# Sums of weight blocks by DMA: spread over the front in smaller pieces, products reordered, sums of F moved to VectorE

## The chip, the cores and the metric

The kernel runs on one core of a Trainium2 chip. The metric is the device time of one execution in microseconds; the time stated is the median of three runs. A separate profiled execution gives the traces.

## The reference

One layer of a hybrid trunk over 512 tokens and 16 learned ones (528 rows, width 1024): an input projection feeds an RWKV-7 recurrence (8 heads of 64), a forgetting attention (8 heads of 64) and gates; then comes an MLP.

```python
u = rmsnorm(h, norm_mix)
proj = u @ w_in
gates = sigmoid(proj[..., C_RW + C_FX:] + b_gate)
y_rw = rwkv7_branch(proj[..., :C_RW], ...)      # S = S*diag(w) + (S a) b^T + v k^T ; y = S r
y_fx = fox_branch(proj[..., C_RW:C_RW + C_FX], ...)  # causal softmax with a decay of F = cumsum(log_f)
merged = gates[..., :D] * (y_rw @ w_out_rw) + gates[..., D:] * (y_fx @ w_out_fx)
h = h + merged @ w_o
z = rmsnorm(h, norm_mlp)
h = h + square(relu(z @ w_up)) @ w_down         # 1024 -> 4096 -> 1024
```

## The kernel before

Every large product is made in three passes: each float32 operand is split into a high part (`whi`, `fhi`, a conversion on ScalarE) and the rest (`wlo`, `flo`, a subtraction on VectorE or GpSimd), and TensorE adds high x high, high x low and low x high.

**The front** (up to about 515 us of the span) does the projections, the recurrence and the attention. A planner (`Turns`, `Clock`) writes the order of TensorE's instructions: several streams (the recurrence's chain, rank 0; its preparation, rank 1; attention, 2; its features, 3; group norms, 4; projections and gates, 8; the sums of the weights, 9) are asked in turn, and the lowest rank whose inputs are due on the planner's clock goes next. TensorE keeps the order so written. The other engines' instructions are ordered by a scheduler, which may take an instruction early if nothing that it reads is missing. The recurrence handles two groups of two head pairs: for each pair keys, `rows`, `scores` (`psr`, L761) and turned keys (`pbt`), then for the group a triangular inverse (`Ain`, `AX`, `tmp`, L784 to L858) and a chain of nine chunks (`pch`, L887 to L919). The projections load a block of weights (`wraw`, two halves of 128x512 from `in_win`, L438), convert it (L447 on ScalarE, L448 on GpSimd) and multiply it (L476); there are four buffers each of `wraw`, `whi` and `wlo`, so two blocks.

**The MLP's second product** is made from 2x2 blocks by Winograd's form of Strassen's scheme: seven products in place of eight. F = square(relu(z w_up)) is cut in four blocks by rows (two of 256 tokens) and by inner index (the halves of a pair of 128 columns); `w_down` into B11, B12, B22, B21. The right factors need four sums of the weights, T1 to T4 (`tsum`), which do not depend on the data: `weight_sums` makes them in HBM by DMA during the front, a copy issued by ScalarE and an accumulating DMA issued by GpSimd for each, in pieces of 512 rows (1 MB): T1 = B11 + B12, T3 = B12 + B22, T2 = B22 + T1, T4 = B21 + T2, in the signs that the blocks hold. The left factors need S1 to S4, sums of blocks of F, made per pair in `left_factors` (L1146 to L1155) by GpSimd.

The inner dimension goes in three slices of 6, 6 and 4 pairs. In each slice the up products (`up_part`, L1138) write F's blocks (`R`, `up_evac`), `left_factors` converts seven left factors (`fhi`, `flo`), and then come seven products over the slice's pairs (L1204): A11 B11, S2 T2, S3 T3, S1 T1, A12 B21, S4 B22, A22 T4. Two of them (`x6`, `x7`) gather in PSUM over all slices (`pd`), two in `v1` and `v5`, and three are added to the result `hres`. In the last slice the gathered ones are combined, with GpSimd adding `v1` and `v5` to `hres` (L1230 to L1239), and the result is stored.

Of the kernel before, what the change touches and what calls it, by code (L numbers as in the profile page):

```python
# [9 lines left out]
F32 = mybir.dt.float32  # L10
# [18 lines left out]
SLICES = (6, 6, 4)  # L29
# [120 lines left out]
class Turns:  # L150
# [4 lines left out]
    ROOM = {0: 0.0, 1: 0.8, 2: 1.5, 3: 1.5, 4: 2.5, 8: 0.5, 9: 0.0}  # L155
# [32 lines left out]
def kernel(ctx, tc, ht, x, win, par, cst, gain, lora, wout, wo, wup, wdn, out, dbg=None):  # L188
# [78 lines left out]
    tsum = [dr.tile([2048, 512], F32, name=f"tsum{i}") for i in range(4)]  # L267

    with ExitStack() as st:
# [136 lines left out]
        opened = act(gf, gf, AF.Tanh, scale=0.5)  # L406
# [592 lines left out]
        def weight_sums():  # L999

            def part(t, c):
                return t[512 * c:512 * c + 512].rearrange("(a b) c -> a (b c)", b=4)

            t1, t2, t3, t4 = tsum
            b11, b12, b22, b21 = (wdn[i] for i in range(4))
            steps = []
            for c in range(4):
                for dst, src in ((t1, b11), (t3, b12), (t2, b22), (t4, b21)):
                    steps.append((dst, src, c, False))
                for dst, src in ((t1, b12), (t3, b22), (t2, t1), (t4, t2)):  # L1010
                    steps.append((dst, src, c, True))
            for n, (dst, src, c, adds) in enumerate(steps):
                yield lambda: 50.0 + 11.0 * n
                if adds:
                    nc.gpsimd.dma_start(part(dst, c), part(src, c), accum_op=ALU.add, max_dma_last_dim=8192)
# [115 lines left out]
    with ExitStack() as st:  # L1131
# [15 lines left out]
        def left_factors(fhi, flo, j, R):  # L1147

            a11, a12, a22, s1, s2, s3, s4, a21 = (R[:, i, :] for i in range(8))
# [4 lines left out]
            A.copy(fhi[:, j], R[:, :7])  # L1154
            V.tensor_tensor(flo[:, j], R[:, :7], fhi[:, j].bitcast(F32), ALU.subtract)  # L1155

        def right_factors(src):

            return [load_h(src[128 * b:128 * b + 128], V, "w", (4, 4, 4)) for b in range(2)]

        A11, A12, A22, S1, S2, S3, S4 = range(7)
        B11, B22, B21, T1, T2, T3, T4 = wdn[0], wdn[2], wdn[3], *tsum
# [4 lines left out]
        p0 = 0  # L1167
        for n_pairs in SLICES:
# [27 lines left out]
            def product(x, left, right, start, stop):  # L1196

                for j in range(0, n_pairs, 2):
                    r0 = 128 * (p0 + j)
                    w = right_factors(right[r0:r0 + 256])  # L1200
                    final = left in (A12, S4, A22) and last and j == n_pairs - 2
                    for i, b in [(i, b) for i in range(2) for b in range(2)] if final else [(i, b) for b in range(2) for i in range(2)]:
                        for n, (a, c) in enumerate(passes((fhi, flo), w[b])):
                            mm(x[i], a[:, j + b, left, 128 * i:128 * i + 128], c, start=start and j + b == 0 and n == 0,  # L1204
                               stop=stop and j + b == n_pairs - 1 and n == 2)

            def gathered(v, left, right):
                x = [ppo() for i in range(2)]
                product(x, left, right, True, True)
                for i in range(2):  # L1210
                    if first:
                        A.copy(v[:, i], x[i])
                    else:
                        V.tensor_tensor(v[:, i], v[:, i], x[i], ALU.add)

            def added(a, b, left, right, op):
                x = [ppo() for i in range(2)]
                product(x, left, right, True, True)
                for i in range(2):
                    h = hr[a][b][:, i]  # L1220
                    V.tensor_tensor(h, h, x[i], op)
                    if last:
                        r0 = 256 * a + 128 * i
                        nc.sync.dma_start(out[r0:r0 + 128, 512 * b:512 * b + 512], h)

            gathered(v1, A11, B11)
            product(x6, S2, T2, first, last)
            product(x7, S3, T3, first, last)
            if last:
                G.tensor_tensor(hr[0][0], hr[0][0], v1, ALU.add)  # L1230
                for i in range(2):
                    V.tensor_tensor(v1[:, i], x6[i], v1[:, i], ALU.subtract)
                G.tensor_tensor(hr[0][1], hr[0][1], v1, ALU.add)
                for i in range(2):
                    V.tensor_tensor(v1[:, i], v1[:, i], x7[i], ALU.subtract)
            gathered(v5, S1, T1)
            if last:
                G.tensor_tensor(hr[0][1], hr[0][1], v5, ALU.subtract)
                G.tensor_tensor(hr[1][0], hr[1][0], v1, ALU.subtract)  # L1239
                for i in range(2):  # L1240
                    h = hr[1][1][:, i]
                    V.tensor_tensor(h, h, v1[:, i], ALU.add)
                    V.tensor_tensor(h, h, v5[:, i], ALU.subtract)
                    r0 = 256 + 128 * i
                    nc.sync.dma_start(out[r0:r0 + 128, 512:], h)
            added(0, 0, A12, B21, ALU.add)
            added(0, 1, S4, B22, ALU.subtract)
            added(1, 0, A22, T4, ALU.add)
            p0 += n_pairs

# [76 lines left out]
```

## Time and profile before

| | us |
|---|---|
| median of three runs | 954.82 (953.65 to 956.38) |
| the profiled execution | 957.5 |
| its span | 955.6 |
| TensorE matmul busy | 866.4 (91%) |
| VectorE busy | 590.1 (62%) |
| ScalarE busy | 460.1 (48%) |
| GpSimd (POOL) busy | 238.3 (25%) |
| mean granted TensorE clock | 0.962 |

In the views PE is TensorE, PEld its weight loads, DVE VectorE, ACT ScalarE, POOL GpSimd, SP the engine that issues most DMAs. A row of the timeline or of the chain of waits has the start in us, the duration in us, and what ran, with "out<-in" by the program's names; in brackets stands the idle time before it and who ended it. A row of the waits has who waited for whom, us in total, times, and the longest. A row of the stages has the stretch and its length, then the busy time of each engine with its number of instructions, the granted TensorE clock, the mean busy share of the 16 DMA engines and GB/s. L12 is line 12 of the kernel.

### The profile page before, as it was taken

What the parts mean: (1) busy time and instruction counts of PE and PEld (TensorE: products, weight loads), DVE (VectorE), ACT (ScalarE), POOL (GpSimd) and SP (SyncE); (2) the same over time, 40 slices, a digit from 0 to 9 for tenths busy, and PEclk for the clock granted to TensorE, in tenths of its full rate; (3) what the DMA queues carried; (4) which work ended last, traced back from release to release, by engine and by line L of the source; (5) the groups of instructions that cost most, each with busy time, mean ns of one, the idle gap of its engine ahead of it and who ended that gap; (6) DMA issues with size and microseconds to landing.
All of it is one profiled execution on the core that took longest, in us unless ns stands there. A gap on an engine that the chain in (4) does not pass through costs nothing.

```text
span 955.6 us, 15670 instructions
## 1 busy us (share of the span) xinstructions
PE 866.4 (91%) x5868; PEld 700.5 (73%) x5868; DVE 590.1 (62%) x1102; ACT 460.1 (48%) x923; POOL 238.3 (25%) x229
## 2 busy tenths in 40 slices
PE   6668794689999989999998999999999999999987
PEld 4566783476788768767686887888788887888865
DVE  7857443745588779446447766446556466564686
ACT  6743531139665553266446554344554444444442
POOL 4244333322244325121210220033200233001341
PEclk9888977799999999999998999999999999999999
DMA  6479999951211114212116654013466323763345
GB/s 204 131 217 279 261 271 251 233 158 35 79 48 57 56 35 139 67 58 79 45 52 234 195 181 155 1 56 110 121 203 192 100 91 88 217 193 109 102 133 185
DMA packets 56971, 129.45 MB, mean 135 GB/s; under 512 B 6328, under 2 KB 7480, under 8 KB 52800
## 3 DMA queue, kind: packets, MB, share of 16 engines
q1 hardware_dynamic: 52288, 94.91, 31.0%
q0 software_dynamic: 2304, 16.78, 9.0%
q10 hardware_dynamic: 2304, 16.78, 4.7%
q8 instruction: 46, 0.75, 0.3%
q14 instruction: 29, 0.24, 0.1%
HBM read 122.13 MB, written 39.86 MB: 170 GB/s over the span
## 4 chain that ended last, share of the span: by engine, by line
PE 61%; DVE 14%; DMA 12%; ACT 5%; issue 4%; POOL 2%; SPq 0%; ACTq 0%; DVEq 0%; POOLq 0%
PE po L1138 18%; PE pj L476 14%; PE po L1204 8%; PE pd L1204 3%; DMA tsum<-in_wdn 3%; DMA wraw<-in_win 3%; PE po L1108 2%; PE po L1059 2%; DMA tsum<-tsum 2%; DVE tmp L810 1%; DVE wlo L236 1%; PE py L625 1%; PE psc L580 1%; PE pw L828 1%; DVE xt L377 1%
## 5 line engine op out<-in xcount | busy, mean ns | idle before, releaser
L236 DVE TENSOR_TENSOR wlo<-wraw,whi 128x512 fp32r<-128x512 f32 x196 | 150.8, 784 | 82.5 <-ACT whi L235 82.2
L235 ACT CAST whi<-wraw 128x512 fp32r<-128x512 f32 x200 | 122.7, 620 | 143.7 <-PE po L1138 58.7
L476 PE MATMUL pj<-uhi,whi 128*128 128x264 f32 (+1 forms) x480 | 172.5, 359 | 15.9 <-ACT gt L487 9.0
L476 PE MATMUL pj<-uhi,wlo 128*128 128x264 f32 (+1 forms) x480 | 159.9, 333 | 17.2 <-POOL wlo L448 17.2
L476 PE MATMUL pj<-ulo,whi 128*128 128x264 f32 (+1 forms) x480 | 159.6, 332 | 0.0
L448 POOL TENSOR_TENSOR wlo<-wraw,whi 128x512 fp32r<-128x512 f32 x80 | 110.8, 1403 | 191.7 <-ACT whi L447 177.2
L476 PEld LDWEIGHTS pj<-uhi,whi 128*128 128x128 f32 x480 | 95.0, 198 | 38.0 <-issue 11.7
L476 PEld LDWEIGHTS pj<-uhi,wlo 128*128 128x128 f32 x480 | 95.2, 198 | 25.6 <-POOL wlo L448 18.1
L476 PEld LDWEIGHTS pj<-ulo,whi 128*128 128x128 f32 x480 | 95.5, 199 | 4.7
L1138 PE MATMUL po<-zhi,whi 128*128 128x512 f32 (+1 forms) x248 | 94.8, 382 | 0.0
L1138 PE MATMUL po<-zlo,whi 128*128 128x512 f32 (+1 forms) x248 | 94.8, 382 | 0.0
L1138 PE MATMUL po<-zhi,wlo 128*128 128x512 f32 (+1 forms) x248 | 94.8, 382 | 0.0
L447 ACT CAST whi<-wraw 128x512 fp32r<-128x512 f32 x80 | 49.0, 618 | 64.9 <-DMA wraw<-in_win 30.4
L1151 POOL TENSOR_TENSOR R<-R 128x256 f32<-128x256 f32 x16 | 16.7, 1044 | 240.7 <-DVE R L1145 240.7
L1204 PE MATMUL po<-wlo,fhi 128*128 128x512 f32 x160 | 62.8, 393 | 5.9 <-DVE wlo L236 5.8
L1204 PE MATMUL po<-whi,fhi 128*128 128x512 f32 x160 | 62.3, 391 | 2.0 <-ACT fhi L1154 1.8
L1204 PE MATMUL po<-whi,flo 128*128 128x512 f32 x160 | 62.1, 389 | 0.0
L1155 DVE TENSOR_TENSOR flo<-R,fhi 128x1792 fp32r<-128x1792 f32 x16 | 32.4, 2026 | 43.4 <-ACT fhi L1154 43.4
L1138 PEld LDWEIGHTS po<-zhi,wlo 128*128 128x128 f32 x248 | 46.6, 188 | 9.1
L1138 PEld LDWEIGHTS po<-zlo,whi 128*128 128x128 f32 x248 | 46.6, 188 | 9.1
L1138 PEld LDWEIGHTS po<-zhi,whi 128*128 128x128 f32 x248 | 46.6, 188 | 8.9
L1154 ACT CAST fhi<-R 128x1792 fp32r<-128x1792 f32 x16 | 27.1, 1696 | 29.7 <-POOL R L1153 29.7
(301 smaller groups left out, 1705.3 us busy)
## 6 DMA issues: line engine op xcount, KB each, us to landing
wraw<-in_win SPq DMA_DIRECT2D x84, 256.0 KB, 3.3
tsum<-in_wdn ACTq DMA_DIRECT2D x16, 1024.0 KB, 9.4
wraw<-in_wup SPq DMA_DIRECT2D x64, 256.0 KB, 2.9
wraw<-tsum SPq DMA_DIRECT2D x64, 256.0 KB, 2.9
wraw<-in_wdn SPq DMA_DIRECT2D x48, 256.0 KB, 2.8
tsum<-in_wdn POOLq DMA_DIRECT2D x8, 1024.0 KB, 17.7
tsum<-tsum POOLq DMA_DIRECT2D x8, 1024.0 KB, 12.5
gd<-gt SPq DMA_DIRECT2D x16, 256.0 KB, 2.2
```

The costliest lines, as they stand in the source:

```text
L235: A.copy(hi, raw)
L236: low.tensor_tensor(lo, raw, hi.bitcast(F32), ALU.subtract)
L447: A.copy(hi, raw)
L448: G.tensor_tensor(lo, raw, hi.bitcast(F32), ALU.subtract)
L476: mm(po, a, b[:, k, a0:a1], start=n == 0, stop=n == 23)
L1059: mm(po, a, b[:, k, :], start=n == 0, stop=n == 11)
L1108: mm(po, a[:, k, 128 * i:128 * i + 128], b[:, k, :], start=n == 0, stop=n == 23)
L1138: mm(po[:, t0:t1], a, b[:, k, t0:t1], start=n == 0, stop=n == 23)
L1151: G.tensor_tensor(s3, a11, a21, ALU.subtract)
L1154: A.copy(fhi[:, j], R[:, :7])
L1155: V.tensor_tensor(flo[:, j], R[:, :7], fhi[:, j].bitcast(F32), ALU.subtract)
L1204: mm(x[i], a[:, j + b, left, 128 * i:128 * i + 128], c, start=start and j + b == 0 and n == 0, stop=stop and j + b == n_pairs - 1 and n == 2)
```

## The change

Four edits are made together.

- The weight sums are issued in pieces of 256 rows (512 KB): 32 copies and 32 accumulating DMAs in place of 16 and 16, with descriptors of 2 KB in place of 8 KB. Each piece is a tensor of its own. A copy and the add that needs it are at least two steps apart. The stream has rank -1, so that each step is written as soon as the planner's clock reaches 45 + 6 n (it was 50 + 11 n at rank 9), and each DMA is tied behind the instruction of its engine that was written last before it (`behind`), so the scheduler can't take it earlier.
- The slices are 4, 6 and 6 pairs.
- In each slice the products that need no sum of F come first: A11 B11, A12 B21, A22 T4, S2 T2, S3 T3, S1 T1, S4 B22. Right factors are loaded one 128-row block at a time, two blocks ahead of the first product.
- The sums of F are made by VectorE, and `fhi` and `flo` are converted in two pieces, the blocks of F first and then the sums. In the last slice the additions to `hres` that GpSimd made go to VectorE, one job at a time between blocks (`soon`, `later`).

```diff
-SLICES = (6, 6, 4)
+SLICES = (4, 6, 6)
+FIRST = (0, 4, 10)
...
-    ROOM = {0: 0.0, 1: 0.8, 2: 1.5, 3: 1.5, 4: 2.5, 8: 0.5, 9: 0.0}
+    ROOM = {0: 0.0, 1: 0.8, 2: 1.5, 3: 1.5, 4: 2.5, 8: 0.5, -1: 0.0}
...
-            ck.urgent = s[0] < 2
+            ck.urgent = 0 <= s[0] < 2
...
-    tsum = [dr.tile([2048, 512], F32, name=f"tsum{i}") for i in range(4)]
+    quarters = [[wdn[i][256 * c:256 * c + 256] for c in range(8)] for i in range(4)]
+    tsum = [[dr.tile([256, 512], F32, name=f"tsum{i}") for c in range(8)] for i in range(4)]
...
+            def behind(dma, engine):
+                x = next(x for x in reversed(nc.cur_bb.bb.instructions) if str(x.engine).endswith(engine) and x.name != dma.ins.name)
+                tc.add_manual_dep(dma.ins, x.name, mybir.DependencyInfo(mybir.DependencyClass.NoSync, mybir.DependencyReason.DATA),
+                                  reason="spread over the front")
...
-            for c in range(4):
-                for dst, src in ((t1, b11), (t3, b12), (t2, b22), (t4, b21)):
-                    steps.append((dst, src, c, False))
-                for dst, src in ((t1, b12), (t3, b22), (t2, t1), (t4, t2)):
-                    steps.append((dst, src, c, True))
+            for c in range(8):
+                for a, b in (((t1, b11), (t1, b12)), ((t3, b12), (t3, b22)), ((t2, b22), (t2, t1)), ((t4, b21), (t4, t2))):
+                    steps += [(*a, c, False), (*b, c, True)]
+            for n in range(1, len(steps) - 2, 2):
+                steps[n], steps[n + 1] = steps[n + 1], steps[n]
             for n, (dst, src, c, adds) in enumerate(steps):
-                yield lambda: 50.0 + 11.0 * n
+                yield lambda: 45.0 + 6.0 * n
                 if adds:
-                    nc.gpsimd.dma_start(part(dst, c), part(src, c), accum_op=ALU.add, max_dma_last_dim=8192)
+                    behind(nc.gpsimd.dma_start(part(dst, c), part(src, c), accum_op=ALU.add, max_dma_last_dim=2048), "Pool")
                 else:
-                    after(nc.scalar.dma_start(part(dst, c), part(src, c), max_dma_last_dim=8192), opened)
-
-        turns.add(9, weight_sums())
+                    behind(nc.scalar.dma_start(part(dst, c), part(src, c), max_dma_last_dim=2048), "Activation")
+
+        turns.add(-1, weight_sums())
...
-            G.tensor_tensor(s1, a22, a21, ALU.subtract)
-            G.tensor_tensor(s3, a11, a21, ALU.subtract)
-            G.tensor_tensor(s2, a11, s1, ALU.add)
-            G.tensor_tensor(s4, s2, a12, ALU.subtract)
-            A.copy(fhi[:, j], R[:, :7])
-            V.tensor_tensor(flo[:, j], R[:, :7], fhi[:, j].bitcast(F32), ALU.subtract)
+            def halves(a, b):
+                A.copy(fhi[:, j, a:b], R[:, a:b])
+                V.tensor_tensor(flo[:, j, a:b], R[:, a:b], fhi[:, j, a:b].bitcast(F32), ALU.subtract)
+
+            halves(0, 3)
+            a11, a12, s1, s2, s4 = (R[:, i, :] for i in (A11, A12, S1, S2, S4))
+            V.tensor_tensor(R[:, S3:S1 + 1, :], R[:, 0:3:2, :], bc(R[:, 7, :], 1, 2), ALU.subtract)
+            V.tensor_tensor(s2, a11, s1, ALU.add)
+            V.tensor_tensor(s4, s2, a12, ALU.subtract)
+            halves(3, 7)
...
+        FACTORS = (A11, B11), (A12, B21), (A22, T4), (S2, T2), (S3, T3), (S1, T1), (S4, B22)
+        AHEAD = 2
+        line = [(right, p0 + j) for p0, n_pairs in zip(FIRST, SLICES) for _, right in FACTORS for j in range(n_pairs)]
...
+                if n == 2 * n_pairs - 1:
+                    fill(AHEAD)
...
-            gathered(v1, A11, B11)
-            product(x6, S2, T2, first, last)
-            product(x7, S3, T3, first, last)
+            gathered(v1, A11)
+            added(0, 0, A12, ALU.add)
             if last:
-                G.tensor_tensor(hr[0][0], hr[0][0], v1, ALU.add)
                 for i in range(2):
+                    soon(lambda i=i: (add(0, 0, i, v1[:, i], ALU.add), store(0, 0, i)))
+            added(1, 0, A22, ALU.add)
+            product(x6, S2, first, last)
...
+            added(0, 1, S4, ALU.subtract, last)
```

More of the change, by code (lines that the diff above doesn't have):

```diff
@@ L1194 @@
             first, last = p0 == 0, p0 + n_pairs == 16
[L1196 to L1205, printed above, removed]
@@ new lines, in own, with gathered, add @@
+            def own(left, end=False):
+                x = [ppo() for i in range(2)]
+                product(x, left, True, True, end)
+                return x
+            def gathered(v, left):
+                for i, x in enumerate(own(left)):
+                    if first:
+                        A.copy(v[:, i], x)
+                    else:
+                        V.tensor_tensor(v[:, i], v[:, i], x, ALU.add)
+            def add(a, b, i, x, op):
+                h = hr[a][b][:, i]
+                V.tensor_tensor(h, h, x, op)
@@ new lines, in store, with added @@
+            def store(a, b, i):
+                r0 = 256 * a + 128 * i
+                nc.sync.dma_start(out[r0:r0 + 128, 512 * b:512 * b + 512], hr[a][b][:, i])
+            def added(a, b, left, op, end=False):
+                for i, x in enumerate(own(left, end)):
+                    add(a, b, i, x, op)
+                    if end:
+                        store(a, b, i)
+            gathered(v1, A11)
+            added(0, 0, A12, ALU.add)
+            if last:
+                for i in range(2):
+                    soon(lambda i=i: (add(0, 0, i, v1[:, i], ALU.add), store(0, 0, i)))
@@ L1240 @@
                 for i in range(2):
[L1241 to L1249, printed above, removed]
+                    soon(lambda i=i: add(0, 1, i, v5[:, i], ALU.subtract))
```

69 lines of the change are left out of this document (40 added, 29 removed).

## The prediction

> **What bounds the kernel now.** I read the page's slices first. In its 40 slices of 23.9 us the granted TensorE clock is below full for the first eight, and the DMA engines are full in the same stretch.
>
> ```profile
> PEclk9888977799999999999998999999999999999999
> DMA  6479999951211114212116654013466323763345
> ```
>
> The table by stages shows what this costs. Its edges are starts of rows on TensorE that occur once for each of the two groups of head pairs (first scores of the group's first pair, first scores of its second pair, first step of its chain), then the up stage and first product stage of the MLP:
>
> ```profile
> 74.83 3.63 PE L761 MATMUL psr<-L,BK 64*128 64x128 f32 x24 [4.78 <-DVE BK L720]
> 118.02 0.46 PE L761 MATMUL psr<-L,BK 64*128 64x128 f32 x2 [0.24 <-DVE BK L720]
> 225.06 0.45 PE L887 MATMUL pch<-uv,L 128*64 128x64 f32 x8
> 285.31 0.94 PE L761 MATMUL psr<-L,BK 64*128 64x128 f32 x12
> 337.78 0.46 PE L761 MATMUL psr<-L,BK 64*128 64x128 f32 x2 [2.29 <-DVE BK L720]
> 414.90 0.45 PE L887 MATMUL pch<-uv,L 128*64 128x64 f32 x8
> ```
> ```profile
> core 0: us, PE busy (x) PEld busy (x) DVE busy (x) ACT busy (x) POOL busy (x), PEclk, DMA share, GB/s
> 74.83:117.95 43.12, 39.10 (x268) 31.70 (x268) 23.23 (x44) 20.47 (x39) 15.67 (x16) 0.89 1.00 278
> 117.95:225.08 107.13, 78.07 (x749) 63.24 (x749) 53.30 (x110) 34.48 (x82) 32.51 (x33) 0.82 0.77 207
> 285.33:337.84 52.51, 48.47 (x390) 41.49 (x389) 43.94 (x105) 28.11 (x70) 20.51 (x16) 1.00 0.17 56
> 337.84:414.93 77.09, 75.36 (x774) 58.53 (x774) 51.76 (x109) 35.14 (x80) 25.50 (x20) 1.00 0.23 75
> 610.00:737.00 127.00, 125.41 (x623) 106.21 (x622) 69.11 (x89) 57.64 (x89) 21.78 (x24) 1.00 0.41 123
> ```
>
> The two groups do the same recurrence work, yet from the second scores to the chain the first takes 107.13 us and the second 77.09, with as many matmul records (749 and 774). In the first, TensorE is busy 73% of the stage at a clock of 0.82, and the DMA share is 0.77 against 0.23. The waits from 30 to 200 us and the chain of waits of that stretch say who holds it:
>
> ```profile
> POOL tsum L1015 <- DMA tsum<-in_wdn: 34.1, 6, 10.9
> POOL tsum L1015 <- DMA tsum<-tsum: 29.1, 4, 15.8
> DVE tmp L810 <- POOL AX L790: 20.7, 1, 20.7
> ```
> ```profile
> 104.84 12.12 DMA wraw<-in_win
> 121.48 17.84 DMA tsum<-in_wdn
> 139.61 17.29 DMA tsum<-tsum
> 158.19 6.60 DVE tmp L810
> ```
>
> POOL stands 63.2 us in front of its own accumulating DMAs, each waiting for an earlier piece of the sums. Behind it in POOL's order are the AX memsets, without which the triangular inverse (`tmp`, L810) cannot begin, and the `wlo` of the projections. A projection's weight load takes 12.12 us at that place; the page's median is 3.3:
>
> ```profile
> wraw<-in_win SPq DMA_DIRECT2D x84, 256.0 KB, 3.3
> ```
>
> From 225 us on TensorE is nearly full, and in the MLP it is full but for the ends of slices. So the front's first 225 us hold what can be won.
>
> **The change part by part.** *The DMAs of the sums.* The order moves instructions on POOL. This is the place of the first inverse's memsets, before:
>
> ```order
> L1015 DMA tsum_90<-tsum_89 128x2048
> L789 MEMSET AX 128x1024
> L1015 DMA tsum_92<-tsum_90 128x2048
> L790 MEMSET AX 128x32
> L448 TENSOR_TENSOR wlo<-wraw,whi 128x512
> L1015 DMA tsum_89<-in_wdn 128x2048
> ```
>
> and the same place in the changed kernel (lines shifted by two, `tsum` numbers are the 32 pieces):
>
> ```order
> L1022 DMA tsum_105<-in_wdn 256x512
> L791 MEMSET AX 128x1024
> L792 MEMSET AX 128x32
> L450 TENSOR_TENSOR wlo<-wraw,whi 128x512 x2
> L1022 DMA tsum_97<-tsum_89 256x512
> L450 TENSOR_TENSOR wlo<-wraw,whi 128x512 x3
> L819 MEMSET AX 128x1152
> L450 TENSOR_TENSOR wlo<-wraw,whi 128x512
> L1022 DMA tsum_113<-tsum_97 256x512
> ```
>
> Before, twelve of the sixteen adds stand ahead of the inverse's second memset; now two of 32 do, of half the size, and the sum of sums (`tsum_97<-tsum_89`) comes behind the memsets. The last copy now stands on ACT just ahead of the last gate's `gt`, at 499.7 us of the trace of before:
>
> ```profile
> L487 ACT ACTIVATE gt<-pj,pr x16: 680/682/691, 180.7 to 499.7; 128x512 f32<-128x512 f32 x16
> ```
>
> TensorE's own order in the front is the same in both kernels up to the first product, so I can price the front by how fast that fixed order is served.
>
> (a) Before 74.83 us. POOL was let go at 68.65 by a landing and then ran piled-up work while VectorE's `BK` (L719) took 4.93 us instead of 0.76:
>
> ```profile
> 68.65 0.83 POOL L1015 DMA_DIRECT2D tsum<-tsum  x1 [7.65 <-DMA tsum<-in_wdn]
> L719 DVE SCALAR_TENSOR_TENSOR BK<-okk,lc x4: 757/757/4931, 69.0 to 336.1; 128x576 f32<-128x576 f32 x4
> ```
>
> TensorE waits 4.78 us for what follows it. No add stands there any more: **-4 us**.
>
> (b) 74.83 to 117.95. TensorE's work at full clock is 39.10 x 0.89 = 34.8 us. At the second group's busy share (48.47/52.51 = 92%) it takes 37.7, so 5.4 less; the 12.12 us load alone would give back 12.12 - 3.3 = 8.8. Bounds 0 and 8; I take **-5**.
>
> (c) 117.95 to 225.08. Work at full clock is 78.07 x 0.82 = 64.0 us; at the second group's busy share (98%) 65.5, a gain of 41.6. By the serial chain the second group's 77.09 us give a gain of 30.0. I take **-34**, nearer to the second row, since the same recurrence runs in it.
>
> (d) What it costs. The sums move the same bytes, and 64 transfers of 512 KB do what 32 of 1 MB did:
>
> ```profile
> q0 software_dynamic: 2304, 16.78, 9.0%
> q10 hardware_dynamic: 2304, 16.78, 4.7%
> ```
>
> 13.7% of the span is 131 us of all 16 engines. Spread from some 100 to 500 us it adds 0.33 to the 0.17 to 0.25 there now: a share near 0.55, no queue full. POOL issues 32 instead of 16, at 0.81 to 1.38 us each, so 13 to 22 us more over a stretch in which it is busy a third of the time: covered. What may not be covered is a wait of POOL, with the `wlo` of the next projection behind it.
>
> ```profile
> L1015 POOL DMA_DIRECT2D tsum<-in_wdn x8: 805/976/1384, 40.4 to 160.8; - x8
> DMA to landing us min/median/max: 8.6/14.1/21.6
> ```
>
> Half of these landings of 1 MB is 4.3, 7.1 and 10.8 us. The cover is the block that TensorE works on: 24 matmuls by 0.23 us (below), 5.5 us, since hi and lo halves of two blocks are held.
>
> ```profile
> 381.96 0.39 PE L476 MATMUL pj<-ulo,whi 128*128 128x512 f32 x1
> 382.20 0.40 PE L476 MATMUL pj<-uhi,wlo 128*128 128x512 f32 x1
> ```
>
> In the order an add stands right behind, or one projection half behind, the add that it reads at five places. Five by 0, 1.6 or 5.3 us is 0, 8 or 26 us; with the DMA share near 0.55 I take 5, and 2 for somewhat later weight loads: **+7**, bounds 0 and 28.
>
> A rule of the Trainium skill speaks against smaller pieces. "DMA: Bandwidth & Descriptors", section "Bandwidth", says to batch transfers to 1 MiB or more, and its section "Anatomy of one DMA — SWDGE (gpsimd) path" gives 2.0 us fixed plus bytes at 436 GB/s. By that an add of 512 KB takes 3.2 us, which the 5.5 us cover, so the +7 would be 0 and the sum 7 us lower; its 2.0 us more for each of 32 added transfers, 64 us of queue time, would lie beside other work. The trace's shortest 1 MB add, 8.6 us, is above the 4.4 that it gives, so I keep the trace's.
>
> *The down stage.* TensorE waits 9.4 us there in all, at the ends of the three slices and in the last one:
>
> ```profile
> PE po L1204 <- DVE wlo L236: 5.8, 4, 2.7
> PE pd L1204 <- DVE wlo L236: 1.8, 2, 1.3
> PE po L1204 <- ACT fhi L1154: 1.8, 1, 1.8
> ```
>
> The order at the end of the last slice on VectorE, before:
>
> ```order
> L1145 SCALAR_TENSOR_TENSOR R<-po,r 128x512
> L236 TENSOR_TENSOR wlo<-wraw,whi 128x512
> L1155 TENSOR_TENSOR flo<-R,fhi 128x1792
> L236 TENSOR_TENSOR wlo<-wraw,whi 128x512
> L1214 TENSOR_TENSOR v_6443<-v_6443,po 128x512 x2
> ```
>
> and now, where `R<-R` are sums that POOL made:
>
> ```order
> L1152 SCALAR_TENSOR_TENSOR R<-po,r 128x512
> L1162 TENSOR_TENSOR R<-R 128x512
> L237 TENSOR_TENSOR wlo<-wraw,whi 128x512
> L1158 TENSOR_TENSOR flo<-R,fhi 128x768
> L1163 TENSOR_TENSOR R<-R 128x256
> L237 TENSOR_TENSOR wlo<-wraw,whi 128x512
> L1164 TENSOR_TENSOR R<-R 128x256
> ```
>
> The first product needs only the first 768 columns, and no longer waits for POOL's sums and a conversion of 1792. VectorE's 2.03 us for 1792 columns, 1.13 ns each, become 0.87 and 1.16; by that the sums of 512, 256 and 256 columns add 0.58 and twice 0.29 us a pair, and up to double if short instructions do not shrink in full: 19 to 37 us over sixteen.
>
> ```profile
> L1155 DVE TENSOR_TENSOR flo<-R,fhi 128x1792 fp32r<-128x1792 f32 x16 | 32.4, 2026 | 43.4 <-ACT fhi L1154 43.4
> 688.01 16.32 PE pd L1204 x72
> ```
>
> For six pairs that is 7 to 14 us on an engine that is busy 69.11 of 127 us: covered by TensorE. At a slice's end the cover is the other pairs' blocks of the first product, 6 matmuls by 16.32/72 = 0.227 us each; the shorter first slice has 3 x 1.36 = 4.1 us, and with that gone a wait of about 1 us comes. In the last slice POOL's additions to the result stretched VectorE beside them, three `wlo` to 3.65 us where one alone takes 0.68:
>
> ```profile
> 921.09 2.79 POOL L1233 TENSOR_TENSOR hres<-hres,v 128x1024 f32<-128x1024 f32 x1 [3.03 <-DVE v L1232]
> 920.93 0.68 DVE L236 TENSOR_TENSOR wlo<-wraw,whi 128x512 fp32r<-128x512 f32 x1
> 921.98 3.65 DVE L236 TENSOR_TENSOR wlo<-wraw,whi 128x512 fp32r<-128x512 f32 x3 [0.37 <-ACT whi L235]
> ```
>
> These go, spread one job to a block. Of 9.4 us I take **-6**, bounds -9 and +3 (a 1 us wait at each slice end and none won). The tail behind the last matmul keeps its form.
>
> *Sum.* The profiled execution took 957.5 us, 955.6 of them the span: 957.5 - 4 - 5 - 34 + 7 - 6 = 915.5. The median of the runs, 954.82, lies 2.7 lower, so **913 us**.
>
> **The rivals.** (1) *The front is tied by its own chain, not by the DMAs.* For it: the second group's stage has 98% of TensorE busy, so its 77 us may hold filler that the first group lacks, and VectorE's order in the front moves a little too. Then half of (b) and (c) is won: about 932. Against it: each long piece of the chain there is a DMA. (2) *TensorE's work alone binds.* All of (b) to 8 and (c) to 41.6, no new wait, 9 in the down stage: 957.5 - 4 - 8 - 41.6 - 9 - 2.7 = 892. (3) *Slower: POOL is held all along.* The 16 adds that read another sum stand in POOL's queue over 400 us; if each holds the next projection's `wlo` for 10.8 us, half the longest landing, 16 x (10.8 - 5.5) = 85 us are lost against 49 won: about 991. It decides from 5.5 + 49/16 = 8.6 us of hold each. Against it: at a share near 0.55 landings should be near the short end, and most have two `wlo` between. (4) *Software DMAs starved by VectorE.* VectorE's busy instructions delay POOL's issue, and each of 32 adds lands late by the span of 0.81 to 1.38, 0.6 us: 19 us, and 932 if none of it is covered. The Trainium skill's "SBUF — State Buffer", section "SBUF: two separate sides", warns that VectorE can keep GpSimd from writing the descriptors of its DMAs; the small scatter of these issues speaks for a small price. (5) *The DMAs stay bunched*: the order shows them apart, so only if ACT and POOL reach them late and together; then the down stage's 6 us remain, 949.
>
> **How the numbers follow.** A measurement of this kernel tells about 0.3%, 2.9 us, from no change. Forecast 0.60, rival 1 0.15, rival 2 0.12, rival 3 0.08 (0.02 of it at its deciding point, where nothing changes), rival 4 0.04, rival 5 0.01. Faster 0.60 + 0.15 + 0.12 + 0.04 + 0.01 = 0.92, same 0.02, slower 0.06. The range takes in rivals 1, 2 and 4 with the bounds of (d): 890 to 938.
>
> **What would show it.** Right: from the second scores to the chain, 70 to 77 us at a clock near 1.0; no wait of `tmp` for AX above 3 us; DMA share 0.4 to 0.6 from 100 to 500 us; under 4 us of waits for `wlo` and `fhi` behind 560. Wrong: POOL waiting for `tsum` over 40 us in all with TensorE waiting for `wlo` between 225 and 500 us, or the stage still above 95 us.

## The result, and the profile after

The changed kernel takes 918.79 us (median of four runs, 918.31 to 919.87) against 954.24 us for the kernel before, measured beside it on the same chip (953.47 to 956.38): a ratio of 0.963, 95% interval 0.961 to 0.965. The forecast was 913 us with a range of 890 to 938. The profiled execution took 918.31 us, 916.5 of them the span.

The two rows of the page of slices, with the granted TensorE clock and the share of the DMA engines, now read:

```profile
PEclk9889988999989899999997999999999999999999
DMA  6122634748464546665686644024632356422465
```

The full stretch of the DMA engines, slices 4 to 8 before, is gone; instead the share goes up and down between 0.3 and 0.8 in slices 5 to 23. The table of stages has the same edges as before: first scores of the first group's first pair, first scores of its second pair, first step of its chain, first output product, first up product, last matmul.

```profile
68.25:105.92 37.67, 34.48 (x269) 28.28 (x269) 25.68 (x42) 21.46 (x40) 16.86 (x16) 1.00 0.35 99
105.92:186.71 80.79, 73.00 (x748) 59.45 (x747) 49.83 (x112) 33.72 (x79) 27.73 (x25) 0.92 0.54 137
186.71:489.90 303.19, 285.76 (x2614) 223.11 (x2613) 198.10 (x500) 162.50 (x406) 103.19 (x94) 0.96 0.61 156
489.90:583.26 93.36, 92.15 (x408) 74.68 (x409) 58.18 (x84) 47.76 (x89) 11.71 (x8) 0.99 0.48 155
583.26:912.16 328.90, 328.79 (x1521) 274.57 (x1519) 213.93 (x326) 153.57 (x242) 0.00 (x0) 1.00 0.43 136
```

The last three of these stretches in the kernel before, which the prediction did not show in this cut:

```profile
225.06:518.06 293.00, 280.23 (x2614) 218.02 (x2613) 195.57 (x499) 162.89 (x406) 82.17 (x69) 0.98 0.22 72
518.06:610.21 92.15, 91.14 (x408) 74.17 (x409) 57.63 (x86) 47.48 (x89) 12.01 (x8) 1.00 0.50 163
610.21:951.70 341.49, 331.63 (x1521) 273.92 (x1519) 203.18 (x254) 149.71 (x226) 68.24 (x68) 1.00 0.43 131
```

Stage by stage, in us of the two spans:

| stage | before | after | measured | forecast |
|---|---|---|---|---|
| (a) up to the first scores | 74.83 | 68.25 | -6.6 | -4 |
| (b) to the second pair's scores | 43.2 | 37.7 | -5.5 | -5 |
| (c) to the first chain | 107.0 | 80.8 | -26.3 | -34 |
| to the first output product | 293.0 | 303.2 | +10.2 | +7 (d) |
| to the first up product | 92.2 | 93.4 | +1.2 | |
| first up product to the last matmul, the down stage among it | 341.5 | 328.9 | -12.6 | -6 |
| behind the last matmul | 3.9 | 4.4 | +0.4 | 0 |
| sum | | | -39.1 | -42 |

The waits of the changed kernel from 100 to 490 us show where GpSimd (POOL) still stands in front of its adds, and those of TensorE in stage (c) show what it waits for:

```profile
POOL tsum L1022 <- DMA tsum<-in_wdn: 35.0, 6, 9.1
...
PE pj L478 <- ACT gt L489: 4.7, 1, 4.7
PE psr L763 <- DVE L L767: 1.2, 1, 1.2
```

No wait of TensorE for `wlo` is listed in either stretch, and the only wait of any engine for POOL there is one of 0.9 us, so POOL's 35 us show nowhere else. Before, TensorE's two long waits in stage (c) were these:

```profile
PE pj L476 <- POOL wlo L448: 14.2, 1, 14.2
PE pj L476 <- ACT gt L487: 9.0, 1, 9.0
```

### The profile page after: what moved, and what is told of

Its sections match the earlier page's. It is cut to its first block, busy times and chain, and to the rows that moved or that the text cites. A ratio compares the mean times of both kernels' runs of the same rounds, so it can differ in the third digit from the quotient of the medians.

```text
span 916.5 us, 15714 instructions
## 1 busy us (share of the span) xinstructions
PE 860.8 (94%) x5868; PEld 699.9 (76%) x5868; DVE 601.1 (66%) x1174; ACT 464.6 (51%) x939; POOL 187.7 (20%) x177
## 3 DMA queue, kind: packets, MB, share of 16 engines
q0 software_dynamic: 8704, 16.78, 11.4%
q10 hardware_dynamic: 8704, 16.78, 5.5%
## 4 chain that ended last, share of the span: by engine, by line
PE 72%; DVE 16%; DMA 4%; ACT 4%; issue 3%; POOL 0%; POOLq 0%; SPq 0%; ACTq 0%; DVEq 0%
PE po L1145 19%; PE pj L478 17%; PE po L1235 12%; PE pd L1235 5%; PE po L1066 2%; PE po L1115 2%; DMA wraw<-in_win 2%; PE pw L830 2%; PE py L627 1%; PE psc L582 1%; DVE tmp L812 1%; DVE AX L824 1%; PE pbt L778 1%; DVE xt L379 1%; PE psr L763 1%
## 5 line engine op out<-in xcount | busy, mean ns | idle before, releaser
L237 DVE TENSOR_TENSOR wlo<-wraw,whi 128x512 fp32r<-128x512 f32 x196 | 138.3, 713 | 95.4 <-ACT whi L236 95.3
L1157 ACT CAST fhi<-R 128x768 fp32r<-128x768 f32 (+1 forms) x32 | 30.2, 944 | 24.2 <-DVE R L1164 13.6
L1158 DVE TENSOR_TENSOR flo<-R,fhi 128x768 fp32r<-128x768 f32 (+1 forms) x32 | 34.8, 1088 | 7.8 <-ACT fhi L1157 7.8
L1235 PEld LDWEIGHTS po<-wlo,fhi 128*128 128x128 f32 x160 | 30.0, 188 | 6.5 <-DVE wlo L237 0.2
```

What stands on the lines that cost most here:

```text
L237: low.tensor_tensor(lo, raw, hi.bitcast(F32), ALU.subtract)
L1157: A.copy(fhi[:, j, a:b], R[:, a:b])
L1158: V.tensor_tensor(flo[:, j, a:b], R[:, a:b], fhi[:, j, a:b].bitcast(F32), ALU.subtract)
L1235: mm(x[i], a[:, k, left, 128 * i:128 * i + 128], c, start=start and k == 0 and n == 0, stop=stop and k == n_pairs - 1 and n == 2)
```

## The experiments

Ten further kernels ran, and the changed kernel and one of the ten once more, in three groups of four on three chips; each ratio is to the kernel before on the same chip, with its 95% interval. The chips differ by a few us, so ratios and stages are compared, and absolute times only within a group. In the edits shown, "..." stands for lines left out.

### The two halves of the change

`front_only` is the kernel before with the new DMAs alone; `SLICES`, `left_factors` and the order of the products are as they were.

```diff
...
-                yield lambda: 50.0 + 11.0 * n
+                yield lambda: 45.0 + 6.0 * n
...
-        turns.add(9, weight_sums())
+        turns.add(-1, weight_sums())
...
```

`down_only` is the changed kernel with the old `weight_sums`.

```diff
...
-                yield lambda: 45.0 + 6.0 * n
+                yield lambda: 50.0 + 11.0 * n
...
-        turns.add(-1, weight_sums())
+        turns.add(9, weight_sums())
...
```

> The kernel before with the change's DMAs of the sums alone; its slices, products and sums of F are those of before. Theory (front and down stage add up, and the front's part by the traces is 26 of 39 us): 926 to 930. Rival (the down stage gains only where the sums come early or where POOL is free, so the parts do not add): under 923 or over 934.

> The changed kernel with the DMAs of the sums as before (16 + 16 of 1 MB, bunched). Theory: the down stage alone, by the two traces, is 12.6 us shorter, so 940 to 943. Rival (the prediction's 6 us, the rest an effect of the front's end): 946 to 950.

`front_only` took 927.41 us, 0.969 (0.963 to 0.976); `down_only` 945.72, 0.988 (0.984 to 0.992). So about 3.1% belongs to the DMAs and 1.2% to the MLP's part; the change has 3.7%, and the two parts add up to it within their intervals. `front_only` came as expected; `down_only` lies between its expectation (940 to 943) and the rival (946 to 950), and its stages decide. They agree with the sum of two parts: in `front_only` stage (c) has the length that it has in the changed kernel,

```profile
103.43:184.04 80.61, 72.71 (x748) 59.22 (x747) 49.84 (x112) 33.73 (x79) 28.00 (x25) 0.92 0.56 137
```

while its 340.9 us from the first up product to the last matmul are like those of before; `down_only` has 108.89 us in stage (c) and 328.72 at the end.

### What the spread transfers still cost

`no_sums` issues none of the 64 transfers and reads blocks of the weights where the sums stood.

```diff
-        turns.add(-1, weight_sums())
...
-        B11, B22, B21, T1, T2, T3, T4 = quarters[0], quarters[2], quarters[3], *tsum
+        B11, B22, B21, T1, T2, T3, T4 = quarters[0], quarters[2], quarters[3], *quarters
```

> The changed kernel without any DMA of the weight sums; the products take blocks of the weights in place of T1 to T4, so the result leaves the sums out. TensorE's order is the same. It prices what the 64 DMAs still cost in the front. Theory (the sums, spread, still slow the later stages, where the trace of the change is 1.7 + 5.9 + 3.4 us longer than that of before): the stages from the group chain of the first group to that of the second go back to 60, 52.5 and 77 us, the stage of the first inverse falls from 81 to about 76, and the time is 902 to 910. Rival (the first inverse's stage and the later ones are bound by the serial chain and by TensorE, the DMAs cost nothing): 916 to 920.

It took 910.46 us, 0.952 (0.947 to 0.958), against the changed kernel's 0.963: by the ratios some 10 us less, by the two spans (909.1, on another chip) 7.4. That is the upper end of the 902 to 910 expected, and the fall of stage (c) to 76 us is not there. Two of its stages, (c) and the one behind it:

```profile
108.16:187.72 79.56, 72.89 (x748) 59.43 (x747) 48.47 (x109) 33.81 (x79) 21.82 (x19) 0.91 0.19 60
...
187.72:483.84 296.12, 284.31 (x2614) 221.12 (x2613) 194.00 (x498) 163.15 (x405) 81.98 (x69) 0.97 0.22 71
```

From the first chain to the output products it needs 296.1 us and the changed kernel 303.2: by this pair the transfers cost 7.1 us there, 5.6 of it idle time of TensorE (17.4 against 11.8, length less busy time) and the rest longer busy time. That is term (d). And stage (c) is hardly shorter without any transfer, 79.6 us: what the change left of it is not the sums' doing. Its longest wait of TensorE there is the same one for `gt`, 4.2 us.

### Is it POOL standing in front of its adds, or the full DMA engines?

`copies_only` is the kernel before with every accumulating transfer replaced by two plain copies of 1 MB into spare memory. They wait for no other transfer, so POOL is never held. The DMA engines carry about the same time, 14.7% of the span against 13.7, but more bunched: POOL's first copy starts at 2.9 us, where its first add in the kernel before starts at 40.4.

```diff
...
-                    nc.gpsimd.dma_start(part(dst, c), part(src, c), accum_op=ALU.add, max_dma_last_dim=8192)
+                    for x in range(2):
+                        nc.gpsimd.dma_start(part(spare.pop(), 0), part(wdn[n % 4], c), max_dma_last_dim=8192)
```

> The kernel before with each accumulating DMA of POOL replaced by two plain copies of 1 MB from the weights into spare tensors: about the same DMA time (48 copies against 16 and 16 of double price), at the same rows of POOL's order, but none waits for another, so POOL is never held by a landing. The sums are left out. Theory A (the loss of the first 225 us comes from POOL being held in front of the memsets and the low halves): most of the front's 26 us come back, 925 to 935. Theory B (it comes from the DMA engines being full, so that weight loads take 12 us): no gain, 948 to 957.

It took 961.09 us, 1.005 (1.001 to 1.009), above even theory B: nothing is won. Its DMA row and stage (c):

```profile
DMA  7699999941211113222115655013376333663345
...
121.88:225.66 103.78, 75.68 (x747) 60.69 (x748) 47.11 (x110) 34.05 (x80) 25.96 (x29) 0.81 0.76 267
```

POOL's waits for `tsum` are gone, and others have come. The waits from 80 to 226 us, and the chain of waits of that stretch:

```profile
ACT whi L448 <- DMA wraw<-in_win: 34.8, 10, 6.2
PE pj L477 <- ACT gt L488: 24.3, 2, 14.5
ACT lw L259 <- DMA lraw<-in_lora: 22.6, 3, 11.2
```
```profile
109.94 13.77 DMA wraw<-in_win
125.78 23.40 DMA wraw<-in_win
153.55 19.66 DMA lraw<-in_lora
173.89 11.91 DMA lraw<-in_lora
```

The chain now runs through the loads that the recurrence and the projections need, which take 12 to 23 us beside the sums' traffic. So the wait that the prediction put first, POOL in front of its own adds, is not needed for the loss: full DMA engines alone make one of the same size, by another way. How the loss of the kernel before divides between the two is not shown by this, since the engines there are less bunched, and what POOL's hold would cost with free DMA engines was not tried.

### Is it the smaller pieces or the spreading?

`untied` keeps the 64 small pieces, the tensor for each and the place in the planner, but not the ties that keep ScalarE and POOL from taking them early.

```diff
-        act(gf, gf, AF.Tanh, scale=0.5)
+        opened = act(gf, gf, AF.Tanh, scale=0.5)
...
-                    behind(nc.gpsimd.dma_start(part(dst, c), part(src, c), accum_op=ALU.add, max_dma_last_dim=2048), "Pool")
+                    nc.gpsimd.dma_start(part(dst, c), part(src, c), accum_op=ALU.add, max_dma_last_dim=2048)
...
-                    behind(nc.scalar.dma_start(part(dst, c), part(src, c), max_dma_last_dim=2048), "Activation")
+                    after(nc.scalar.dma_start(part(dst, c), part(src, c), max_dma_last_dim=2048), opened)
```

> The changed kernel without the ties: the same 64 small pieces, the same place in the planner's order and the same order on TensorE, but ScalarE's and GpSimd's instructions may be taken early; 24 of the 32 adds then stand ahead of the first inverse's memsets. If it is the spreading that wins, as I hold, most of the front's 38 us is lost again: the first scores to the chain 95 to 108 us, the time 940 to 948. Rival: the small pieces, each a tensor of its own, are enough, since an add of 512 KB lands in half the time; then 80 to 84 us there and 919 to 925 in all.

It took 963.91 us, 1.005 (1.001 to 1.008), more than either expectation. Its DMA row, its two stages (b) and (c), and two of its waits from 127 to 241 us:

```profile
DMA  6499999891211111313113665203553346623465
...
64.07:127.30 63.23, 40.95 (x270) 33.00 (x269) 27.08 (x45) 21.66 (x41) 32.38 (x33) 0.81 0.98 234
127.30:240.77 113.47, 79.45 (x748) 62.36 (x748) 55.54 (x110) 33.70 (x80) 36.60 (x38) 0.80 0.78 189
...
DVE tmp L812 <- POOL AX L792: 22.2, 1, 22.2
PE pj L478 <- POOL wlo L450: 19.5, 4, 15.6
```

The gain of the MLP's part is still there (329.2 us), and the front is 17.6 us longer than before (535.7 to the first output product against 518.1). Without the ties the small pieces come together again, and are worse than the large ones were; the spreading carries the whole gain of the front. POOL's hold is back in this run too (22.2 us of `tmp`), beside the full engines.

`whole_pieces` goes the other way: spread and tied as in the change, but 32 transfers of 1 MB.

```diff
-    tsum = [[dr.tile([256, 512], F32, name=f"tsum{i}") for c in range(8)] for i in range(4)]
+    tsum = [[dr.tile([512, 512], F32, name=f"tsum{i}") for c in range(4)] for i in range(4)]
...
-                yield lambda: 45.0 + 6.0 * n
+                yield lambda: 45.0 + 12.0 * n
...
```

> The changed kernel with the sums in 16 + 16 transfers of 1 MB in place of 32 + 32 of 512 KB, spread and tied over the same stretch (45 + 12 n), descriptors of 2 KB. Theory (what counts is that the DMA engines are not full; the spread does that): within 4 us of the change, 916 to 923. Rival (the small piece matters: while a 1 MB transfer runs, a weight load behind it doubles, and POOL is held twice as long where an add reads the one before it): 925 to 935.

It took 921.19 us, 0.961 (0.956 to 0.967): as expected, the ratio of the change within its interval. One row of its page:

```profile
tsum<-tsum POOLq DMA_DIRECT2D x8, 1024.0 KB, 9.6
```

The Trainium skill's rule to batch to 1 MiB or more ("DMA: Bandwidth & Descriptors", section "Bandwidth"), which the prediction weighed, neither gains nor costs here: bandwidth is not what is short once the transfers are spread.

### Half of the transfers later

`late` issues the first 32 transfers in the front at 45 + 12 n, and the other 32 one by one at the blocks of the MLP's up products.

```diff
-            for n, (dst, src, c, adds) in enumerate(steps):
-                yield lambda: 45.0 + 6.0 * n
+            late.extend(lambda s=s: issue(*s) for s in steps[32:])
+            for n, s in enumerate(steps[:32]):
+                yield lambda: 45.0 + 12.0 * n
+                issue(*s)
...
+                late.pop(0)()
```

> The changed kernel with only the first half of the pieces (pairs 0 to 7) in the front, at 45 + 12 n, and the other half issued one step to an up block of the MLP, where POOL has no other work. The result is the same. Theory (in the front a step costs about 8/64 us, in the up stages TensorE has all its weights well ahead): half of the 8 us come back, 912 to 916. Rival (the up stages' weight loads come late when the DMA share there goes from 0.24 to 0.6): 919 or more, with waits for wlo in the up stages.

It took 913.39 us, 0.951 (0.945 to 0.957). To take the chip out of it, it ran again, unchanged, beside the changed kernel itself:

> The changed kernel once more, as the yardstick for the other three of this call: 917 to 921 us, and 65 to 70, 37 to 39, 79 to 83 us in the first three stages of the front.

> The kernel that leaves half of the sums' transfers for the up blocks of the MLP, against the changed kernel on one chip. If the transfers are what the front still loses (8 us for all 64 by the kernel without them), half of them gone from it gains 2 to 6 us on the changed kernel of this call, in the stages behind the first chain, and the MLP stays within 1 us. If the gain seen before was the chip's, the two agree within 1.5 us.

`after_again` took 920.32 us, 0.960 (0.956 to 0.964; six runs, 917.71 to 921.54), and `late_again` 914.48, 0.954 (0.950 to 0.958; six runs, 913.17 to 916.38). The runs do not overlap: half of the transfers in the MLP is worth another 5.8 us, and it beats both kernels. The DMA row shows the load moved behind slice 26, into the MLP:

```profile
DMA  6122326335532346334366646078667776577575
```

Where the 5.8 us come from is not settled. The profiled executions of the two, 917.71 and 914.66 us, differ by less than the medians, and their spans' 3.0 us are scattered over the stages: 1.0 in (b) and (c) together, 2.0 up to the first output product.

### The MLP's part, taken apart

`sums_first` puts three of the four products that need sums of F back behind the first product, much as they stood, and keeps the rest of the change. `pool_sums` keeps the new order and gives the four sums back to GpSimd, with one conversion of 1792 columns for each pair. `pool_adds` lets GpSimd add `v1` and `v5` to the result in the last slice, still one job between blocks.

```diff
-        FACTORS = (A11, B11), (A12, B21), (A22, T4), (S2, T2), (S3, T3), (S1, T1), (S4, B22)
+        FACTORS = (A11, B11), (S2, T2), (S3, T3), (S1, T1), (A12, B21), (A22, T4), (S4, B22)
...
```
```diff
...
-            halves(0, 3)
...
-            halves(3, 7)
+            G.tensor_tensor(s1, a22, a21, ALU.subtract)
...
+            A.copy(fhi[:, j], R[:, :7])
+            V.tensor_tensor(flo[:, j], R[:, :7], fhi[:, j].bitcast(F32), ALU.subtract)
```
```diff
-                V.tensor_tensor(h, h, x, op)
+                (G if any(x.tensor.name == v.tensor.name for v in (v1, v5)) else V).tensor_tensor(h, h, x, op)
```

> The changed kernel with the products in an order like that of before (after A11 B11 those of S2, S3 and S1, then A12, A22 and S4); the sums of F on VectorE, converted in two pieces. Theory (the down stage's 12.6 us come mainly from the sums leaving POOL, with the additions to the result; the order hides only the sums' own chain of some 3 us at each slice end, with 4 to 7 us of the first product's blocks over it): within 2 us of the change, 917 to 921. Rival (the order is what hides the sums): 2 us at each slice end and more at the last, 924 to 930.

> The changed kernel with the sums of F on POOL and one conversion of seven factors a pair, as before; the order of products and the additions on VectorE are those of the change. Theory (POOL's sums and the long conversion stand between the last up block and the first product): 2 us at each of three slice ends, 3 us more at the short one, so 924 to 928. Rival (only the additions in the last slice cost): 917 to 920.

> The changed kernel with one part of its last slice undone: v1 and v5 are added to the result on GpSimd again, still one job between blocks. If GpSimd's work beside VectorE is what stretched the weight conversions at the end, the down stage grows by 2 to 5 us (3.65 us for three conversions in the trace of before against 0.68 for one alone, twice or more), 920 to 924 us in all. Rival: it was the bunching of these jobs, not the engine; then the time is that of the changed kernel within 1 us.

From the first up product to the last matmul, in this order, with the changed kernel run again as the last row:

```profile
584.50:915.38 330.88, 329.84 (x1521) 274.33 (x1519) 213.85 (x326) 153.51 (x242) 0.00 (x0) 1.00 0.45 136
```
```profile
582.55:920.74 338.19, 332.29 (x1521) 275.31 (x1519) 199.95 (x262) 149.46 (x226) 57.61 (x64) 0.99 0.44 133
```
```profile
576.85:908.36 331.51, 329.72 (x1521) 274.39 (x1519) 217.01 (x314) 153.53 (x242) 18.74 (x12) 1.00 0.45 135
```
```profile
581.68:911.57 329.89, 329.22 (x1521) 274.50 (x1519) 213.81 (x326) 153.42 (x242) 0.00 (x0) 1.00 0.45 136
```

Against the changed kernel's two traces, 328.9 and 329.9 us, the order is worth 1.0 to 2.0 us, and the sums on VectorE with the conversion in two pieces 8.3 to 9.3. The additions on VectorE are worth 1.6 against the 329.9 of their own chip. In all, `sums_first` took 921.97 us (0.962, 0.956 to 0.967), `pool_sums` 926.27 (0.966, 0.960 to 0.971) and `pool_adds` 919.03 (0.959, 0.953 to 0.965), which is 1.3 us below the changed kernel of its group: the expected 2 to 5 us are not there, and the 1.6 us of the stage are no more than hinted at. Which of the two, GpSimd's sums or the long conversion, makes the 8.3 to 9.3 us was not separated; in `pool_sums` TensorE's listed waits are 3.8 us for `wlo` and 1.8 for `fhi`. One effect that goes with GpSimd's work can be read, though: from 583 us on, a `wlo` on VectorE takes 689 ns on average where GpSimd does nothing (the changed kernel and `sums_first`), 745 in `pool_sums`, 751 in `pool_adds` and 778 before. The new sizes of the slices and the loading by single blocks were not undone alone.

## Why the prediction was right, and where it was not

**What bounds the kernel** was right: the first 225 us held what could be won in the front, and the bunched DMAs were the reason. How they cost the time was put too narrowly. The step "POOL stands 63.2 us in front of its own accumulating DMAs" was named first and the late weight load second; `copies_only` shows that with POOL free the late loads alone cost as much.

**The total** is nearer to the forecast than its terms. Term (c), the stage up to the first output product and the one behind it came out 12.1 us dearer than forecast, and (a), (b) and the down stage 9.7 cheaper; that these nearly cancel is luck. With 0.4 us behind the last matmul they leave 2.9 us of the 5.8 by which the forecast was low. Another 2.7 us had been taken off for the step from the profiled execution to the median, and that step did not come again (918.31 and 918.79).

**(a) and (b)** came out at -6.6 and -5.5 against -4 and -5. For (b) the second group's busy share gave 37.7 us, and 37.67 were measured, at a clock of 1.00. That it agrees to the digit is luck: other kernels with the same order on TensorE need 40.8 to 40.9 us there, as is shown below.

**(c) was too high**, -26.3 against -34: of its two bounds, TensorE's work (-41.6) and the second group's 77.09 us (-30.0), the measured gain lies below both. The failed step is to take it that the first group's stage can be served as the second's is, with TensorE busy for 98% of it at full clock. The first keeps one wait that the second lacks, and its clock falls. (The bound by work was too generous as well: busy time by clock, 64.0 us before, comes to 73.00 x 0.92 = 67.2 in the changed kernel for the same matmuls, so that product is no fixed amount of work.) The changed kernel's timeline shows the wait on ScalarE and on TensorE:

```profile
152.66 0.30 ACT L260 CAST lw<-lraw 128x128 fp32r<-128x128 f32 x1 [6.72 <-DMA lraw<-in_lora]
153.40 0.62 ACT L449 CAST whi<-wraw 128x512 fp32r<-128x512 f32 x1 [0.44 <-DMA wraw<-in_win]
153.92 0.68 ACT L489 ACTIVATE gt<-pj,pr 128x512 f32<-128x512 f32 x1
```
```profile
154.66 0.79 PE L478 MATMUL pj<-uhi,whi 128*128 128x512 f32 x1 [4.69 <-ACT gt L489]
155.25 0.63 PE L478 MATMUL pj<-ulo,whi 128*128 128x512 f32 x1
...
160.53 0.39 PE L478 MATMUL pj<-ulo,whi 128*128 128x512 f32 x1
```

ScalarE stands 6.72 us for a small load; the gate's `gt` is queued behind it, and TensorE waits 4.69 us for `gt`. Then its matmuls run slower until 160 us. The windows on either side say by how much:

```profile
150.00:155.00 5.00, 0.34 (x1) 0.35 (x2) 0.76 (x2) 1.90 (x4) 0.91 (x1) 0.85 0.40 131
155.00:160.00 5.00, 5.00 (x34) 3.18 (x33) 0.94 (x6) 1.12 (x3) 1.85 (x3) 0.50 0.70 249
160.00:186.00 26.00, 25.10 (x432) 20.40 (x428) 12.07 (x37) 15.60 (x40) 7.45 (x8) 0.99 0.70 164
```

The granted clock is 0.50 in the 5 us right behind the idle time: 2.5 us of work lost on top of 4.7 us of waiting, 7.2 us that term (c) did not look at. The Trainium skill has the rule: in "TensorE: Matmul & The Clock Gate", Part 1, the array runs at half its clock after an idle window and is released by a window of sustained work. The trace agrees here, with 0.50 and then 0.99. Term (c) had only to notice that the 9.0 us wait for `gt` in the trace of before was not all the sums' doing: `no_sums` has 4.2 us of it with no transfer at all.

The stage has a second slow spell, and this one moves from run to run. The first 20 us of the stage in the changed kernel and in `late_again`:

```profile
105.92:125.00 19.08, 17.07 (x131) 14.71 (x131) 12.60 (x27) 4.50 (x13) 5.33 (x6) 0.82 0.43 113
```
```profile
108.12:128.00 19.88, 18.92 (x173) 16.30 (x173) 15.85 (x38) 8.52 (x20) 6.19 (x7) 1.00 0.44 97
```

`late_again`, with 4.9 us of the same wait for `gt`, has the whole stage (c) in 76.5 us; but its stage (b) ran at a clock of 0.92 and took 40.8 us in place of 37.7. `late`, the same kernel, has the slow spell in (c): 37.8 and 80.6 us. `no_sums` has one in both stages (40.9 and 79.6), `whole_pieces` too (40.9 and 80.3), `pool_adds` in neither (37.8 and 76.8). So (b) is known to some 3 us, (c) to 4, and their sum to between 114.6 and 121.2 us, 118.5 in the changed kernel. Of the 7.7 us by which (c) fell short, this spell is worth some 4, since `late_again` and `pool_adds` fall short by 3.4 and 3.7 with the same wait in them. The wait and the slow matmuls behind it come to 7.2 by themselves, so the two do not add up to 7.7: the -34 was chosen between bounds and left some room, and an exact account of the miss cannot be made.

The Trainium skill's same section calls the gate's window free-running and the number of slow matmuls run-variable; that the spell's place differs between `late` and `late_again`, one kernel on two chips, fits that. What does not fit is an idle window as its condition: in the changed kernel the clock is 1.00 from 70 to 110 us and 0.76 and 0.56 in the next two 5 us, and the longest idle time of TensorE between 98 and 114 us is 1.9 us, where the other spell had 4.69 ahead of it. The measurement decides here: an idle time that long is not needed. What sets the spell off and places it was not tested.

**(d)** was right in size, as far as that is known: +7 was forecast, and the cost is 7.1 us by `no_sums` and 10.2 against the kernel before. Without transfers of the sums in it, this stage took 290.8 us in `down_only`, 293.0 before, 296.1 in `no_sums` and 296.2 in `copies_only`, so one trace tells it to some 5 us; what makes this scatter is open. The make-up of (d) was not right. Five held adds were to cost 5 of it; no wait of TensorE for `wlo` is listed behind POOL's waits of 35.0 us, and the cost is idle time of TensorE, in short waits, and a lower clock (0.96 against 0.97).

**The down stage was too low**, -12.6 against -6 with a bound of -9. Two steps failed. The waits listed, 9.4 us, were taken for all that could be won; but TensorE's idle time in that stretch was 9.9 us before (341.49 less 331.63) and is 0.1 now, and busy time fell by a further 2.8 us for the same 1521 matmuls. Ends of matmuls are modelled, 0.39 us long at a spacing of 0.23, so a short wait vanishes inside a row. And the waits that were to come at the slices' ends, 1 us each, did not: behind 560 us no wait of TensorE for `wlo` or `fhi` is listed, and its weight loads have one of 0.2 us for `wlo` and one for `flo`.

**The signs it named**: waits for `wlo` and `fhi` behind 560 us under 4 us, no `tmp` wait for AX, POOL waiting less than 40 us (35.0; 43.7 in `after_again`, also without a wait of TensorE for `wlo`), and a DMA share of 0.59 from 100 to 500 us, at the top of the forecast 0.4 to 0.6, came as said; stage (c) at 70 to 77 us and a clock near 1.0 did not. **Of the rivals**, the first (the front's own chain) is the one with a part in it: a wait that no transfer of the sums makes is still there and (c) falls short by 7.7 us, where half of (b) and (c), 19.5 us, was priced. The 892 us of rival 2 were out of reach: without any transfer `no_sums` still takes 910. POOL's holds did not reach TensorE (rival 3), and the DMAs did not stay bunched (rival 5), but `untied` shows that rival 5 without the ties is real and costs more than its 949 us. For rival 4 little is seen: with VectorE 66% busy POOL's issues took 0.86 to 1.20 us, no longer than the 0.81 to 1.38 before, and the adds of 512 KB landed in 6.7 to 7.4 us at the median.

## What to carry to other kernels

Background transfers are worth spreading and tying to a place in the order of the engine that issues them: the scheduler of this kernel, where it may take them early, bunches them, and the loads that the critical chain needs then come late, whether or not the issuing engine is held. Before pricing a stage by a twin stage, list the waits of the compute engine in it and ask of each whether the change removes its cause; one that stays costs its length and, here, the slow clock behind it. Before reading a stage's last few us, take the trace of the same kernel twice: here one stage differed by 4 us. For TensorE compare the length of a stage with the spacing of its matmuls rather than the list of its waits, which counts too little.

## What the runs showed of the hardware

An accumulating transfer from HBM to HBM took the DMA engines about twice as long as a copy of the same bytes: before, 16.78 MB took 9.0% as adds and 4.7% as copies, and in `copies_only` 33.56 MB of plain copies from the same queue took 9.8%. In the changed kernel, with descriptors of 2 KB in place of 8 KB, the same adds and copies take more:

```profile
q0 software_dynamic: 8704, 16.78, 11.4%
q10 hardware_dynamic: 8704, 16.78, 5.5%
```

That is 105 us of all engines in place of 86 for the adds, with 3.8 times the packets. The size of the pieces is not the main reason: `whole_pieces`, with the same descriptors in pieces of 1 MB, has 8448 packets and 10.7% of its span, 99 us. A landing depends on the company as well as on the size: adds of 512 KB took 6.7 to 7.4 us at the median in the changed kernel and 8.0 to 9.7 in `untied`, and spread adds of 1 MB 9.6 to 10.5 where bunched ones, in the kernel before and with its larger descriptors, took 12.5 to 17.7.

The trace's record of the granted clock has it at half or at full, and every slow spell of the changed kernel that ends within the span lasts a multiple of 3.41 us. The one behind the wait of 4.69 us lasts 6.83, so it outlives the wait by 5.7.
